# Weight splits written behind the chains of a tile, and five of 16 chunks of three modulation vectors moved from VectorE to TensorE's column groups

## The chip, the core and the metric

The kernel is one program on one core of a Trainium2 chip. The metric is the device time of one execution in microseconds, here the median of three runs. The engines have short names in the profile: PE is TensorE's matrix multiply and PEld its weight load, DVE is VectorE, ACT is ScalarE, POOL is GpSimd, SP issues the loads. Each engine works through its own queue of instructions in order. An instruction may wait for others by semaphores, and while it waits all that stand behind it on its engine wait too.

## What is computed

One layer of a network on 256 tokens of width 2048, in float32. Cut to what matters here:

```python
c_act = silu(c)
mod = c_act @ w_ada + b_ada                     # six vectors of 2048: 0 to 5
sh_m, sc_m, gt_m, sh_f, sc_f, gt_f = split(mod, 6)
h = rms_norm(x, g_norm_mix) * (1 + sc_m) + sh_m             # uses 1 and 0
b_g, c_g, h_c, q_lat, kv_lat, k_rope = split(h @ w_in)
conv_out = b_g * causal_conv3(c_g * h_c)
attn_out = mla_attention(q_lat, kv_lat, k_rope, ...)        # low-rank q and kv, 8 heads
merged = concat(group_rms_norm(conv_out), group_rms_norm(attn_out))
x = x + gt_m * (merged @ w_out)                             # uses 2
h2 = rms_norm(x, g_norm_ffn) * (1 + sc_f) + sh_f            # uses 4 and 3
x = x + gt_f * peer_ffn(h2)                                 # most of the time
return rms_norm(x, g_final)
```

## The kernel before

**Products.** A weight tile is 128 x 2048 numbers, 1 MB. It is split into a high part (`hi`, by ACT, line 198) and the rest (`lo`, by DVE, line 199), and a product is made of three: the high weights with the high and the low activations, then the low weights with the high activations (`mm3`, lines 213, 214 and 217). For a tile of 16 blocks that is a chain of 32 + 16 matmuls of 128 x 256. `load_split` does the load and the split. Its raw buffers (`wraw`, four) are shared with the chunks below; `hi` and `lo` have two buffers each, so that the split of a tile has to wait until the tile two before it has been used up: the `hi` buffer comes free two thirds into a chain, the `lo` buffer at its end.

**Stages.** The first 141 us make vectors 1 and 0 and the first twelve tiles of `w_in`, interleaved (`ada_q`, `unit`). Then come the tiles of the first convolution group, with the norms of the two latents between them (`lat_chain`: `ssl`, `rl0r`, `rlb0` for q, `ssl`, `rl1r`, `rlb1` for kv); the latent products `puq`, `puk`, `puv`; the mixer, 18 tiles `pwin` in six convolution groups (`conv_group`), with attention (`attend`) and the group norms (`conv_norm`: `cn0`, `cn1`) started at given tiles by `AGENDA` (the trace leaves numbers out: its `at_4pn` and `at_4on` are those of query half 1, heads 4 and 5); then `w_out`, 16 chains `pwout`, the first two interleaved with the norm `cn2`, each followed by its eviction (`wout_evict`) and scaling (`wout_scale`); the norm of the result (`x1ss`, `n1b`), and from 470 us on the query projection and the experts, which the diff doesn't touch. The tiles of a convolution group stand in the order 2, 3, 1 of it, so that the mixer's last three are tiles 19, 20 and 18.

**A norm** (`rstd_cols`, lines 340 to 349) is a row of short steps that go from PE's sums to DVE (`v`), to ACT (square root, `r`), and back to DVE for four steps (lines 345 to 348); PE then spreads the result (`rstd_bc`).

**Vectors 2, 4 and 3** come from `ada_stream`: 16 chunks each of 1 MB. Each chunk is multiplied with its 16th of `c_act` and added up on DVE in `acc` (`ada_acc`, line 241). After the last, four matmuls with ones sum over the partitions (`adaps`, in column groups of 32), ACT copies the row (`adarow`), four more matmuls turn it (`adacol`), and DVE adds the bias. `feed` takes one step of this stream whenever `PACE`, 46 chunks in 41 tiles, has added up to one, and it lets the waiting generators (norms, attention) go on by one step (`tick`).

**Order.** A scheduler orders each engine's instructions by the order in which they are written; `high_priority(offset=60)` in `load_split` moves the two split instructions ahead by that much.

Of the kernel before, what the change touches and what calls it, by code (L numbers as in the profile page):

```python
# [57 lines left out]
ADA_LAST = (0, 1, 1)  # L58
PACE = (48 - sum(ADA_LAST)) / 41.0
# [71 lines left out]
def hybrid_block_kernel(  # L131
# [100 lines left out]
    def ada_acc(acc, m, k, pool=None):  # L232
        if pool is None:
            raw = load_raw(w_ada[m - 2, k], f"ada{m}_{k}")
        else:
            raw = pool.tile([128, 2048], F32, tag="ar", name=f"ada{m}_{k}", bufs=ARBUFS)
            nc.sync.dma_start(raw, w_ada[m - 2, k])
# [4 lines left out]

    with tc.tile_pool(name="pre", bufs=1) as pre:
# [136 lines left out]
        pace = [0.0]  # L380
# [47 lines left out]

        def proj(src, nt, rhs, nm, sets=None):
# [3 lines left out]
            feed(PACE)  # L433
            return p[:, :256]
# [85 lines left out]
        def conv_group(g, ps=None):  # L520
# [8 lines left out]
            V.tensor_scalar(y, z[:, 0:256], vcol("conv_w", g), None, ALU.mult)  # L529
# [910 lines left out]
```

## Time and profile before

| | us |
|---|---|
| median of three runs | 1761.83 |
| the runs | 1760.68, 1761.83, 1767.35 |
| the profiled execution | 1762.56 |
| its span in the profile | 1760.8 |
| PE busy in it | 1683.4 |
| DVE busy | 1200.5 |
| ACT busy | 761.6 |

The profiled execution is the one in which the trace was taken; its span is the time from the first to the last recorded instruction, and what lies around it is 1.8 us. Busy time is the time in which an engine had an instruction at work. The idle time of an engine that isn't the bound costs nothing, so what counts is where PE stands idle, what it waited for, and what clock it had. PEclk is the granted share of the full clock: 1.00 is 2.4 GHz, 0.50 is 1.2 GHz.

### The profile page before, as it was taken

The numbers are of one execution on the slowest core, as the hardware profiler recorded it, in microseconds if no ns is written. First come the engines' busy times: TensorE is split into PE (matmuls) and PEld (weight loads), VectorE is DVE, ScalarE is ACT, GpSimd is POOL, SyncE is SP. The second block draws the span as 40 slices with busy tenths as digits, with TensorE's granted clock in tenths as the row PEclk, the third lists the DMA queues.
The fourth block names the chain that finished last, engine by engine and source line by source line (L and its number), as shares of the span: only waits on it lengthen the run. The fifth ranks groups of instructions, "written<-read, shape, count | busy, mean of one in ns | idle before, by whom it ended". The sixth has DMA issues, their size and how long they took to land. (4 is left out here: it accounts for less than half of the span.)

```text
span 1760.8 us, 29506 instructions
## 1 busy us (share of the span) xinstructions
PE 1683.4 (96%) x12507; PEld 1461.9 (83%) x12507; DVE 1200.5 (68%) x1605; ACT 761.6 (43%) x1016; POOL 288.1 (16%) x257
## 2 busy tenths in 40 slices
PE   4998999899999999999999999999999999999996
PEld 2778999899899999899999999999999754444542
DVE  6769899778667988897885788898744332222324
ACT  3233467334544468847974343333433232222322
POOL 0000000000000000000000000000030476756771
PEclk8988999899999999999999999999999999999998
DMA  9998888679555455546569887888988599998895
GB/s 396 425 375 298 324 331 304 244 277 348 207 217 180 158 182 212 195 175 219 198 233 347 284 307 255 296 298 286 322 311 317 219 393 393 354 361 336 307 395 217
DMA packets 77928, 505.93 MB, mean 287 GB/s; under 512 B 9472, under 2 KB 10112, under 8 KB 22496
## 3 DMA queue, kind: packets, MB, share of 16 engines
q1 hardware_dynamic: 44784, 319.82, 48.2%
q0 software_dynamic: 29712, 162.94, 25.3%
q10 hardware_dynamic: 3296, 21.24, 3.0%
q8 instruction: 100, 1.64, 0.4%
q14 instruction: 36, 0.29, 0.0%
HBM read 466.21 MB, written 37.75 MB: 286 GB/s over the span
## 5 line engine op out<-in xcount | busy, mean ns | idle before, releaser
L213 PE MATMUL pu<-h2hi,hu 128*128 128x256 f32 x2048 | 497.8, 284 | 0.0
L198 ACT ACTIVATE hu<-ru 128x2048 fp32r<-128x2048 f32 x128 | 245.4, 1917 | 365.7 <-PE pu L214 316.7
L213 PEld LDWEIGHTS pu<-h2hi,hu 128*128 128x128 f32 x2048 | 386.0, 188 | 0.6 <-issue 0.2
L199 DVE TENSOR_TENSOR lu<-ru,hu 128x2048 fp32r<-128x2048 f32 x128 | 293.1, 2291 | 135.6 <-ACT hu L198 133.4
L217 PE MATMUL pu<-h2hi,lu 128*128 128x256 f32 x2048 | 263.2, 281 | 0.5 <-DVE lu L199 0.5
L217 PEld LDWEIGHTS pu<-h2hi,lu 128*128 128x128 f32 x2048 | 251.3, 188 | 0.7 <-DVE lu L199 0.7
L214 PE MATMUL pu<-h2loT3a,hu 128*128 128x256 f32 x1024 | 249.4, 282 | 0.0
L214 PE MATMUL pu<-h2loT3b,hu 128*128 128x256 f32 x1024 | 247.9, 281 | 0.0
L1228 PE MATMUL po<-rv,mc 128*64 128x512 f32 (+2 forms) x1064 | 225.5, 600 | 5.2 <-PEq L1310 2.6
L1228 PEld LDWEIGHTS po<-rv,mc 128*64 128x64 f32 (+2 forms) x1064 | 72.6, 131 | 147.0 <-issue 140.5
L214 PEld LDWEIGHTS pu<-h2loT3a,hu 128*128 128x128 f32 x1024 | 193.2, 189 | 0.2 <-issue 0.2
L214 PEld LDWEIGHTS pu<-h2loT3b,hu 128*128 128x128 f32 x1024 | 192.9, 188 | 0.0
L1125 POOL DMA_DIRECT2D gg<-gd x16 | 18.7, 1169 | 914.9 <-DVE work L1002 914.6
L1170 POOL DMA_INDIRECT rv<-in_peer_v_dram,perm_idx x107 | 129.1, 1207 | 77.1 <-PE po L1228 33.2
L204 DVE TENSOR_TENSOR lv<-rv,hv 128x2048 fp32r<-128x2048 f32 x24 | 55.1, 2294 | 122.5 <-ACT hv L203 89.9
L1177 POOL DMA_INDIRECT mc<-actd,perm_idx x109 | 121.1, 1111 | 37.1 <-issue 30.8
L241 DVE SCALAR_TENSOR_TENSOR acc<-ada,cact,acc 128x2048 f32<-128x2048 f32 x45 | 105.7, 2348 | 3.4 <-DMA ada<-in_w_ada_dram 3.4
L203 ACT ACTIVATE hv<-rv 128x2048 fp32r<-128x2048 f32 x24 | 45.9, 1913 | 130.6 <-DMA rv<-in_peer_v_dram,perm_idx 118.4
L198 ACT ACTIVATE hwin<-rwin 128x2048 fp32r<-128x2048 f32 x33 | 63.0, 1910 | 66.1 <-DMA rwin<-in_w_in_dram 40.0
L213 PE MATMUL pwin<-hhi,hwin 128*128 128x256 f32 x336 | 88.4, 301 | 0.0
L872 ACT ACTIVATE oh<-oh,gT 128x128 f32<-128x128 f32 x256 | 80.8, 390 | 14.8 <-DVE oh L869 14.1
L204 DVE TENSOR_TENSOR third<-rv,third 128x2048 fp32r<-128x2048 f32 x12 | 27.6, 2299 | 87.3 <-ACT third L203 53.7
(522 smaller groups left out, 3036.3 us busy)
## 6 DMA issues: line engine op xcount, KB each, us to landing
ru<-in_peer_u_dram SPq DMA_DIRECT2D x128, 1024.0 KB, 5.4
ada<-in_w_ada_dram SPq DMA_DIRECT2D x96, 1024.0 KB, 7.4
rwin<-in_w_in_dram SPq DMA_DIRECT2D x33, 1024.0 KB, 6.1
rwout<-in_w_out_dram SPq DMA_DIRECT2D x16, 1024.0 KB, 5.3
rwq<-in_w_q_dram SPq DMA_DIRECT2D x16, 1024.0 KB, 4.8
gd<-stage ACTq DMA_DIRECT2D x16, 1024.0 KB, 5.0
gg<-gd POOLq DMA_DIRECT2D x16, 1024.0 KB
actd<-A POOLq DMA_DIRECT2D x15, 1024.0 KB
```

The lines of the kernel that those rows point to most:

```text
L198: S.activation(hi, raw, AF.Copy)
L199: V.tensor_tensor(lo, raw, hi.bitcast(F32), ALU.subtract)
L203: S.activation(hi, src, AF.Copy)
L204: V.tensor_tensor(lo, src, hi.bitcast(F32), ALU.subtract)
L213: PE.matmul(dst, lhsT=whi[:, sl], rhs=rhi[:, c], start=(c == sets[0][0]), stop=False)
L214: PE.matmul(dst, lhsT=whi[:, sl], rhs=rlo[:, c], start=False, stop=False)
L217: PE.matmul(dst, lhsT=wlo[:, sl], rhs=rhi[:, c], start=False, stop=(c == sets[-1][-1]))
L241: V.scalar_tensor_tensor(acc, raw, cact[:, k:k + 1], acc, ALU.mult, ALU.add)
L872: S.activation(ohs[1][:, j], ohs[1][:, j], AF.Copy, scale=gT[:, t + j:t + j + 1])
L1170: keep(nc.gpsimd.indirect_dma_start(raw, None, v_rows, index(main[n])))
L1177: keep(nc.gpsimd.indirect_dma_start(ms[-1][:, n % 8], None, actd[:, :], index(main[n])))
L1228: keep(PE.matmul(po[tt * 4 + d4][row:row + size], lhsT=m[:, at * size:(at + 1) * size], rhs=raw[:, d4 * 512:(d4 + 1) * 512], start=start, ...
```

## The change

**Chunks.** Of the 16 chunks of each vector, the five in `ADA_PE3` are no longer multiplied on DVE. PE does them in the four column groups of the tile `adaps`, four matmuls of 128 x 512 a chunk, and the sum of the other eleven (`acc` times ones) is added into the same tile. That tile is one of eight PSUM buffers and is now held from the vector's beginning to its end. The pace goes by stage, and one chunk less is taken before the first convolution tiles.

**Splits.** The tiles after the first stage stand in a list (`todo`), and `split_next`, called in `feed` behind a chain and behind `tick`, writes the next load and split, two tiles ahead, with no offset in the order.

**Moved steps.** The first tap of the convolution and the scaling by `r` in attention go from DVE to ACT; the square of the last `w_out` column goes from ACT to DVE.

```diff
-ADA_LAST = (0, 1, 1)
-PACE = (48 - sum(ADA_LAST)) / 41.0
+ADA_LAST = (0, 0, 1)
+ADA_PE3 = (2, 5, 8, 11, 14)
+PACES = {"start": 0.67, "latent": 1.0, "mixer": 1.1, "out": 1.4}
...
-        def ada_finish(m, acc):
-            p = ps_tile(f"adaps{m}")
-            by_columns(p, ones[:, 0:32], acc, True, True)
+        def ada_finish(m, acc, p):
+            by_columns(p, ones[:, 0:32], acc, stop=True)
...
                 acc = t8(f"acc{m}", shape=(128, 2048))
+                p = ps_tile(f"adaps{m}")
                 for k in range(16):
-                    ada_acc(acc, m, k, pre if ARBUFS else None)
+                    raw = load_raw(w_ada[m - 2, k], f"ada{m}_{k}")
+                    if k in ADA_PE3:
+                        by_columns(p, cact[:, k:k + 1].to_broadcast([128, 32]), raw, start=(k == ADA_PE3[0]))
+                    else:
+                        ada_acc(acc, raw, k)
...
-        def feed(x):
+        def feed(n=1, ahead=1):
             tick()
-            pace[0] += x
+            for _ in range(ahead):
+                split_next()
+            pace[0] += n * pace[1]
...
+        def split_next():
+            if todo:
+                src, j, nm = todo.pop(0)
+                ready.append((src, j, load_split(src[j], f"{nm}{j}", 0)))
...
         def proj(src, nt, rhs, nm, sets=None):
-            w = load_split(src[nt], f"{nm}{nt}")
+            w = weights(src, nt)
...
-            V.tensor_scalar(y, z[:, 0:256], vcol("conv_w", g), None, ALU.mult)
+            S.activation(y, z[:, 0:256], AF.Copy, scale=vcol("conv_w", g))
...
-                V.tensor_scalar(on[:, gs_], po[:, gs_], r[:, g:g + 1], None, ALU.mult)
+                S.activation(on[:, gs_], po[:, gs_], AF.Copy, scale=r[:, g:g + 1])
...
         conv_group(0, [pin_nt(9 + i) for i in range(3)])
+        split_next()
+        split_next()
         conv_group(1)
...
-            S.activation(sq[:, :256], xt[:, dt], AF.Square)
+            if dt == 15:
+                V.tensor_tensor(sq[:, :256], xt[:, dt], xt[:, dt], ALU.mult)
+            else:
+                S.activation(sq[:, :256], xt[:, dt], AF.Square)
...
-                feed(2 * PACE)
+                feed(2, 0)
+        for dt in range(2):
+            split_next()
```

The order of the instructions shows the effect at three places. The first is DVE at the norm of the q latent, behind the last chains of the first stage; `lwin` is the low half of a tile's split, `acc` a chunk, `z` the convolution's product. Before:

```order
L199 TENSOR_TENSOR lwin_1226<-rwin_1223,hwin_1225 128x2048 [waits DMAHW5_49,Activation_49]
L345 RECIPROCAL rl0r<-rl0r 128x2 [waits Activation_49]
L472 TENSOR_TENSOR krT<-kraw,rope_t 128x256 [waits Activation_49]
L346 SCALAR_TENSOR_TENSOR rl0v<-rl0v,rl0r 128x2 [waits DVE_49]
L526 MEMSET z_1215 128x2
L241 SCALAR_TENSOR_TENSOR acc_1136<-ada_2_1295,cact,acc_1136 128x2048 [waits DMAHW6_49]
L347 TENSOR_TENSOR rl0v<-rl0v,rl0r 128x2 [waits DVE_49]
L527 TENSOR_TENSOR z_1215<-cs_1213,pin_179 128x256 [waits Activation_49]
L348 SCALAR_TENSOR_TENSOR rl0r<-rl0v,rl0r 128x2 [waits DVE_49]
```

After, on DVE at the same place (line numbers of the changed kernel):

```order
L342 TENSOR_SCALAR rl0v<-ssl_1116 128x2 [waits PE_49]
L200 TENSOR_TENSOR lwin_1223<-rwin_1220,hwin_1222 128x2048 [waits DMAHW4_49,Activation_49]
L345 RECIPROCAL rl0r<-rl0r 128x2 [waits Activation_49]
L475 TENSOR_TENSOR lacc_1130<-lsq_1129 128x256 [waits Activation_49]
L346 SCALAR_TENSOR_TENSOR rl0v<-rl0v,rl0r 128x2 [waits DVE_49]
L494 TENSOR_TENSOR krT<-kraw,rope_t 128x256 [waits Activation_49]
L347 TENSOR_TENSOR rl0v<-rl0v,rl0r 128x2 [waits DVE_49]
L476 TENSOR_TENSOR lacc_1130<-lacc_1130 128x256
L348 SCALAR_TENSOR_TENSOR rl0r<-rl0v,rl0r 128x2 [waits DVE_49]
```

Before, a chunk stands between the second and the third step of `rl0r`; now no chunk and no split stands between its steps on DVE behind the reciprocal.

The second place is DVE at the norm `cn1`, in the mixer's last group. `lwin_3277` before and `lwin_3221` after are the low half of the same tile, 18; its buffer is that of tile 19, whose chain is the last on PE ahead of `cn1b`. Before:

```order
L199 TENSOR_TENSOR lwin_3206<-rwin_3203,hwin_3205 128x2048 [waits DMAHW4_49,Activation_49]
L639 SCALAR_TENSOR_TENSOR mg1lo<-at_6pn,vec,mg1hi 128x128 [waits Activation_49]
L345 RECIPROCAL cn1r<-cn1r 128x4 [waits Activation_49]
L346 SCALAR_TENSOR_TENSOR cn1v<-cn1v,cn1r 128x4 [waits DVE_49]
L347 TENSOR_TENSOR cn1v<-cn1v,cn1r 128x4 [waits DVE_49]
L639 SCALAR_TENSOR_TENSOR mg1lo<-at_6pn,vec,mg1hi 128x128 [waits Activation_49]
L348 SCALAR_TENSOR_TENSOR cn1r<-cn1v,cn1r 128x4 [waits DVE_49]
L199 TENSOR_TENSOR lwin_3277<-rwin_3274,hwin_3276 128x2048 [waits DMAHW6_49,PE_49,Activation_49]
```

After, on DVE at the same place:

```order
L345 RECIPROCAL cn1r<-cn1r 128x4 [waits Activation_49]
L237 SCALAR_TENSOR_TENSOR acc_2453<-ada_10_3224,cact,acc_2453 128x2048 [waits DMAHW1_49,DVE_49]
L346 SCALAR_TENSOR_TENSOR cn1v<-cn1v,cn1r 128x4 [waits DVE_49]
L200 TENSOR_TENSOR lwin_3221<-rwin_3218,hwin_3220 128x2048 [waits DMAHW0_49,PE_49,Activation_49]
L347 TENSOR_TENSOR cn1v<-cn1v,cn1r 128x4 [waits DVE_49]
L548 MEMSET z_3289 128x2
L348 SCALAR_TENSOR_TENSOR cn1r<-cn1v,cn1r 128x4 [waits DVE_49]
L527 SCALAR_TENSOR_TENSOR ym<-ym,vec,cn1b_3209 128x256 [waits PE_49]
```

The split stood behind the last step of `cn1r`, and now stands ahead of its last two.

The third place is ACT at the end of `w_out`. `hwout12` to `hwout15` are the high halves of the last splits, `xs1` the scaling of a column (`xs` in the trace), `x1sq` its square. A scaling that waits for DVE waits for an eviction (`xt`). Before:

```order
L745 ACTIVATE xs1_3343<-xt_97,modc_76 128x256
L738 ACTIVATE x1sq11_4117<-xt_97 128x256 [waits DVE_49]
L745 ACTIVATE xs1_3343<-xt_97,modc_76 128x256
L198 ACTIVATE hwout13_4198<-rwout13_4196 128x2048 [waits DMAHW4_49,PE_49,Activation_49]
L306 ACTIVATE adarow3_4188<-adaps3_4183 128x512 [waits PE_49]
L738 ACTIVATE x1sq12_4191<-xt_97 128x256 [waits DVE_49]
L745 ACTIVATE xs1_3343<-xt_97,modc_76 128x256
L198 ACTIVATE hwout14_4265<-rwout14_4263 128x2048 [waits DMAHW5_49,Activation_49]
L198 ACTIVATE hwout15_4326<-rwout15_4324 128x2048 [waits DMAHW6_49,DVE_49,PE_49]
L738 ACTIVATE x1sq13_4258<-xt_97 128x256 [waits DVE_49]
```

After, on ACT at the same place:

```order
L768 ACTIVATE x1sq11_4172<-xt_97 128x256 [waits DVE_49]
L775 ACTIVATE xs1_3356<-xt_97,modc_76 128x256
L775 ACTIVATE xs1_3356<-xt_97,modc_76 128x256 [waits DVE_49]
L199 ACTIVATE hwout13_4164<-rwout13_4162 128x2048 [waits DMAHW1_49,PE_49,Activation_49]
L199 ACTIVATE hwout14_4228<-rwout14_4226 128x2048 [waits DMAHW3_49,PE_49,Activation_49]
L775 ACTIVATE xs1_3356<-xt_97,modc_76 128x256 [waits DVE_49]
L199 ACTIVATE hwout15_4310<-rwout15_4308 128x2048 [waits DMAHW6_49,PE_49,Activation_49]
L301 ACTIVATE adarow3_4245<-adaps3_3579 128x512 [waits PE_49]
L768 ACTIVATE x1sq12_4248<-xt_97 128x256
L768 ACTIVATE x1sq13_4315<-xt_97 128x256
```

`hwout13` stood behind the scaling of column 8 or 9 and now stands behind one that waits for the eviction of chain 12; `adarow3` stood behind `hwout13` and now stands behind `hwout15`. On PE, `adaps3` stood behind chain 12 and `adacol3` behind chain 13; now eight matmuls of `adaps3` (chunk 14 and the finish) stand behind chain 13, and `adacol3` directly behind them, ahead of chain 14. On PE the eight matmuls of `adaps4` now stand between `cn2b` and the first product of the norm, where before nothing stood.

## Rows read from the trace of the kernel before

**Rows 1.** The page: busy us, share of the span, instructions of each engine.

```profile
PE 1683.4 (96%) x12507; PEld 1461.9 (83%) x12507; DVE 1200.5 (68%) x1605; ACT 761.6 (43%) x1016; POOL 288.1 (16%) x257
```

**Rows 2.** Windows of PE: stretch, us, busy of five engines, PEclk, DMA share, GB/s.

```profile
143.75:150.57 6.82, 6.64 (x31) 6.68 (x32) 6.24 (x12) 1.15 (x2) 0.00 (x0) 0.50 0.62 227
157.40:160.81 3.41, 3.41 (x18) 3.41 (x17) 3.41 (x8) 0.68 (x1) 0.00 (x0) 0.50 0.95 372
250.00:300.00 50.00, 50.00 (x416) 49.59 (x416) 47.24 (x75) 32.79 (x68) 0.00 (x0) 1.00 0.83 308
311.01:317.83 6.82, 6.82 (x34) 6.82 (x34) 5.62 (x14) 2.01 (x9) 0.00 (x0) 0.50 1.01 410
324.65:331.48 6.83, 5.69 (x26) 5.72 (x27) 6.39 (x12) 1.01 (x2) 0.00 (x0) 0.50 0.73 270
372.44:379.27 6.83, 5.70 (x28) 5.40 (x27) 6.83 (x6) 4.30 (x4) 0.00 (x0) 0.50 0.58 208
```

**Rows 3.** Timeline of PE: start, us, engine, line, operation, tiles, count, [idle before <-releaser].

```profile
143.93 1.20 PE L354 MATMUL rlb<-ident,rl0r 128*128 128x128 f32 x4 [2.67 <-DVE rl0r L348]
...
156.41 0.68 PE L354 MATMUL rlb<-ident,rl1r 128*128 128x128 f32 x4 [2.65 <-DVE rl1r L348]
...
178.08 0.70 PE L469 MATMUL qr10sw<-qraw,perm 128*128 128x256 f32 x2 [1.15 <-ACT qraw L546]
...
310.00 0.33 PE L634 MATMUL at_4pn<-ident,at_4on 128*128 128x128 f32 x1 [2.37 <-DVE at_4on L626]
...
325.79 1.62 PE L354 MATMUL cn0b<-ident,cn0r 128*128 128x128 f32 x6 [3.82 <-DVE cn0r L348]
...
370.66 0.50 PE L754 MATMUL pwout<-mg0hi,hwout 128*128 128x256 f32 x2 [1.63 <-ACT mg0hi L203]
...
460.69 0.60 PE L337 MATMUL x1ss<-ones,sacc 128*128 128x1 f32 x4 [3.11 <-DVE sacc L742]
```

**Rows 4.** Timeline of DVE ahead of `rl0r`'s last steps.

```profile
140.96 2.35 DVE L241 SCALAR_TENSOR_TENSOR acc<-ada,cact,acc 128x2048 f32<-128x2048 f32 x1
```

**Rows 5.** Timeline of DVE ahead of `cn0b`.

```profile
322.81 2.28 DVE L199 TENSOR_TENSOR lwin<-rwin,hwin 128x2048 fp32r<-128x2048 f32 x1
325.01 0.16 DVE L347 TENSOR_TENSOR cn0v<-cn0v,cn0r 128x8 f32<-128x8 f32 x1
...
325.49 0.16 DVE L348 SCALAR_TENSOR_TENSOR cn0r<-cn0v,cn0r 128x8 f32<-128x8 f32 x1
```

**Rows 6.** Timeline of ACT ahead of `cn0r`'s square root.

```profile
320.12 1.92 ACT L198 ACTIVATE hwin<-rwin 128x2048 fp32r<-128x2048 f32 x1 [6.60 <-PE pwin L214]
```

**Rows 7.** Timeline of PE: the group of `adaps` between two chains of `w_out`.

```profile
438.58 1.07 PE L299 MATMUL adaps<-acc,ones 128*32 128x512 f32 x8
439.57 0.39 PE L213 MATMUL pwout<-mg0hi,hwout 128*128 128x256 f32 x1
439.80 0.28 PE L214 MATMUL pwout<-mg0lo,hwout 128*128 128x256 f32 x1
```

**Rows 8.** Timeline of DVE: evictions in `w_out`, each at the end of its chain.

```profile
404.93 0.48 DVE L736 SCALAR_TENSOR_TENSOR xt<-pwout,modc,xt 128x256 f32<-128x256 f32 x1 [0.34 <-PE pwout L217]
...
410.56 0.48 DVE L736 SCALAR_TENSOR_TENSOR xt<-pwout,modc,xt 128x256 f32<-128x256 f32 x1 [0.34 <-PE pwout L217]
...
438.69 0.48 DVE L736 SCALAR_TENSOR_TENSOR xt<-pwout,modc,xt 128x256 f32<-128x256 f32 x1 [0.28 <-PE pwout L217]
...
445.49 0.48 DVE L736 SCALAR_TENSOR_TENSOR xt<-pwout,modc,xt 128x256 f32<-128x256 f32 x1 [0.34 <-PE pwout L217]
```

**Rows 9.** Timeline of ACT in `w_out`.

```profile
439.71 0.60 ACT L306 ACTIVATE adarow<-adaps 128x512 f32<-128x512 f32 x1 [3.50 <-PE adaps L299]
...
440.51 0.50 ACT L745 ACTIVATE xs<-xt,modc 128x256 f32<-128x256 f32 x1
440.91 1.91 ACT L198 ACTIVATE hwout<-rwout 128x2048 fp32r<-128x2048 f32 x1
```

**Rows 10.** The page's DMA issues: KB each, us from issue to landing.

```profile
ada<-in_w_ada_dram SPq DMA_DIRECT2D x96, 1024.0 KB, 7.4
```

More of the change, by code (lines that the diff above doesn't have):

```diff
@@ L230, in rstd_of, with ada_acc @@
         return r
[L232 to L237, printed above, removed]
+    def ada_acc(acc, raw, k):
         if k == 0:
@@ L379, in hybrid_block_kernel @@
         ada = ada_stream((2, 4, 3))
-        pace = [0.0]
-        def feed(x):
+        pace = [0.0, PACES["start"]]
+        def feed(n=1, ahead=1):
             tick()
-            pace[0] += x
+            for _ in range(ahead):
+                split_next()
+            pace[0] += n * pace[1]
             while pace[0] >= 1.0:
@@ L427, in ada_q, with tiles, groups, weights @@
                 yield
+        def tiles():
+            def groups(gs):
+                return [(w_in, 3 * g - 3 + i, "win") for g in gs for i in (1, 2, 0)]
+            return (groups((1,)) + [(w_uq, j, "wuq") for j in (2, 0, 1)] + [(w_ukv, j, "wukv") for j in range(4)] +
+                    groups(range(2, 8)) + [(w_out, j, "wout") for j in range(16)])
+        todo = tiles()
+        ready = []
+        def split_next():
+            if todo:
+                src, j, nm = todo.pop(0)
+                ready.append((src, j, load_split(src[j], f"{nm}{j}", 0)))
+        def weights(src, j):
+            got = ready.pop(0)
+            assert got[0] is src and got[1] == j
+            return got[2]
         def proj(src, nt, rhs, nm, sets=None):
-            w = load_split(src[nt], f"{nm}{nt}")
+            w = weights(src, nt)
             p = ps_tile(f"p{nm}{nt}")
             mm3(p[:, :256], w, rhs, 16, sets=sets)
-            feed(PACE)
+            feed()
             return p[:, :256]
@@ L534, in uq_tile @@
         def uq_tile(j):
-            w = load_split(w_uq[j], f"wuq{j}")
+            w = weights(w_uq, j)
             for n2 in range(2):
@@ L548, in uq_tile @@
                         spawn(rope(qrT[:, i0 - 8 + i], raw[:, i * 256:(i + 1) * 256], f"qr{i0 + i}"))
-            feed(PACE)
+            feed()
         def uk_tile(j):
-            w = load_split(w_ukv[j], f"wuk{j}")
+            w = weights(w_ukv, j)
             for n2 in range(2):
@@ L559, in uk_tile @@
                 S.activation(knT[:, i0:i0 + 2], pv, AF.Copy)
-            feed(PACE)
+            feed()
         def uv_tile(j):
-            whi, wlo = load_split(w_ukv[2 + j], f"wuv{j}")
+            whi, wlo = weights(w_ukv, 2 + j)
             for tt in range(2):
@@ L574, in uv_tile @@
                 S.activation(vt[:, tt, j * 512:(j + 1) * 512], p, AF.Copy)
-            feed(PACE)
+            feed()
         ATT_SCALE = float(192 ** -0.5)
@@ L717, in hybrid_block_kernel @@
         vt = pre.tile([128, 2, 1024], F32, tag="t8", name="vt", bufs=6)
+        pace[1] = PACES["latent"]
         for j in (2, 0, 1):
@@ L725, in hybrid_block_kernel @@
         agenda.update(AGENDA(attend, conv_norm))
+        pace[1] = PACES["mixer"]
         for g in range(2, 8):
             conv_group(g)
+        pace[1] = PACES["out"]
         drain()
@@ L745, in wout_scale @@
             S.activation(xs1[:, dt], xt[:, dt], AF.Copy, scale=modc[:, 4, dt:dt + 1])
-        ws = [load_split(w_out[dt], f"wout{dt}") for dt in range(2)]
+        ws = [weights(w_out, dt) for dt in range(2)]
         pw = [ps_tile(f"pwout{dt}") for dt in range(2)]
```

2 lines of the change are left out of this document (1 added, 1 removed).

## The prediction

> **What bounds the kernel now.** I read the busy shares first: PE is busy for 96% of the span [rows 1], so work given to PE is paid in full unless it falls into a wait of PE. The changed code ends at the query projection, 470 us into the program; behind it nothing moves. So I read the stretch from 140 to 470 us by its windows. In a window like 250 to 300 us PE is busy for all 50 us at a clock of 1.00 [rows 2]: no relief of DVE or ACT can gain anything there. What can be gained lies in two things. First the waits: the timeline of PE shows four that the change touches, 2.67 us before `rlb0`, 2.37 before `at_4pn`, 3.82 before `cn0b`, 1.63 before the first `mg0hi` product, together 10.5 us [rows 3]. Second, what follows each: at or just behind each of these waits stands a stretch of 6.8 us with PEclk 0.50, which is the lower of the two levels (1.2 GHz). PE is busy in these for 6.64, 6.82, 5.69 and 5.70 us [rows 2], and half of that is lost: 3.3 + 3.4 + 2.8 + 2.9 = 12.4 us. The wait of 1.15 us before `qr10sw` [rows 3] has no such stretch behind it.
>
> All these waits have one form: a short DVE or ACT step that PE waits for stands in its engine's queue behind a long one. Before `rlb0` it is a chunk of the modulation stream, 2.35 us [rows 4]. Before `cn0b`, ACT's split `hwin` stood idle 6.60 us for a buffer [rows 6], with the square root of `cn0r` behind it, and then DVE's `lwin` (322.81 to 325.01) stood ahead of `cn0r`'s last steps [rows 5].
>
> **What the change takes away.** By the order of the changed kernel, no chunk and no split stands any more between the last steps of `rl0r`, the product of `at_4on` is on ACT, `cn0r`'s root stands ahead of the split on ACT, and the wait at `cn2b` holds eight matmuls of `adaps4`. I take all four waits as gone, with the stretches behind them: 10.5 + 12.4 = 22.9 us gained. The 15 chunks that leave DVE free 15 x 2.35 = 35 us of it, but beyond the four waits that buys nothing, since PE doesn't wait there. The first tap of the convolution and the attention products cost ACT what they free on DVE; neither is late for PE elsewhere, so I put them at nothing. The loads on SP are as many as before, and the finish of each vector (a group of `adaps`, four `adacol`) is paid in both kernels.
>
> **What it adds on PE.** 15 groups of four matmuls. The trace has three groups of this form, `adaps`, there with the ones vector. The group at 438.58 us is followed at 439.57 by the next chain, 0.99 us later, and that chain's second matmul comes 0.23 us behind its first, where 0.12 is usual (a chain of 48 in 5.63 us) [rows 7, 8]: 1.1 us a group. The other measure is DVE's evictions: from one chain to the next 5.63 us (404.93 to 410.56), and 6.80 (438.69 to 445.49) with a group between [rows 8], so 1.17. The ends are 15 x 1.0 = 15.0 and 15 x 1.17 = 17.6 us; I take 15 x 1.1 = 16.5. A gain is excluded, as PE has no other wait for them to lie in but the one at `cn2b`, counted above.
>
> The Trainium skill (TensorEngine Tiling (Array Packing), Key Properties) says that a change of tiling mode, not just of tile, drains the TensorE; that speaks against groups set in among full-width chains. The trace agrees as far as the 0.1 us behind the group goes. If the drain were two whole matmuls of 0.28 us in place of 0.12, the groups would cost 15 x 1.3 = 19.8 us, and the sum would be 3 us more.
>
> **What it adds as waits.** The splits are now written right behind the chain before, so that some stand ahead of short steps where before they stood behind them.
> - `cn1b`: DVE's `lwin` of tile 18 waits for the end of chain 19 (its buffer), and `cn1r`'s last two steps now stand behind it; `cn1b` is next on PE. In rows 5 the same row of steps runs from `lwin`'s start at 322.81 to `cn0r` at 325.49 with one other step in it, and 0.30 later PE goes on [rows 3]. So 2.7 us idle (2.3 to 3.2).
> - Chain 13 of `wout`: ACT's `hwout13` stands behind a scaling that waits for the eviction of chain 12. Eviction about 0.5 [rows 8], scaling to split 0.40 and the split 1.91 [rows 9], a hand-over of 0.1: 2.9 us idle (2.4 to 3.5).
> - Behind chain 13: `adaps3`'s last group needs the chunk 15 on DVE, which stands behind the eviction (0.4), `lwout14` (2.3 [rows 5]) and takes 2.35 itself: 5.0 us. Then the group 1.0, `adarow` 0.13 later and 0.60 long [rows 7, 9], then `adacol`, which PE now has ahead of chain 14: 6.8 us, of which 2.1 are work (chunk 14 and the finish). So 4.7 us idle. In the kernel before, a whole chain lay between `adaps3` and `adacol`. ACT has `hwout15`, which waits for its load, ahead of `adarow`: 4.0 to 6.5.
> - `rlb1`: idle 2.65 now [rows 3]. With `rlb0` on time, DVE has two splits (2.3 each), four latent products (0.5 each, like an eviction), a low half of about 1.2 by the split's rate, a first chunk (at most 2.35) and small steps to do, 10 to 11 us, against a chain of 5.6 and 1.1 of small products on PE: 3.3 to 4.3. I take 3.9, 1.2 more.
> - `x1ss` [rows 3]: the square of column 15 now stands on DVE behind `lwq`, ahead of the sum: 0.4 more.
>
> That is 2.7 + 2.9 + 4.7 + 1.2 + 0.4 = 11.9 us idle. The waits of 2.37 us and more in rows 3 each have a stretch at the lower level: 3.1 us lost in the mean of four, 1.7 where another had ended 7 us before (157.40 [rows 2]). For `cn1b` and chain 13 I take 3.0 each, for the end of `wout`, close behind chain 13, 1.7, and 1.3 more at `rlb1`, which loses its near neighbour: 9.0 us (0 to 12).
>
> **The sum.** 16.5 + 11.9 + 9.0 - 22.9 = +14.5 us on the profiled execution's 1762.56, thus 1777; this execution is 0.7 us over the median of the runs, so 1776. Its own range, from the ends of the terms, is 1771 to 1782.
>
> **The rivals.**
> - The clock stays up at the new waits. For it: the 1.15 us before `qr10sw` left it at 1.00. Against: each wait over 2.3 us in rows 3 has its stretch. Then 9.0 us less: 1767, no change that can be told. It decides from the point where two of the three new places keep the clock: 6 us less is 1770. This is the one that ends on the other side, not slower.
> - The new waits are shorter than the order says, because DVE and ACT, with 35 us less on DVE, come to those places early and only the buffer's release counts. Without them, idle and clock, 20.9 us less: 1755; with groups at 1.0 us and a little more, under 1753. Against: the step that counts in each waits for PE's own chain, so an early engine gains nothing.
> - PE waits for loads. Now 15 places of PE, not of DVE, wait for a chunk; a chunk takes 7.4 us to land [rows 10], the DMA share is already 0.83 at 250 to 300 us [rows 2], and one PSUM buffer of eight is held all the time. At half a microsecond a place, +8: 1784. Against: the chunk's load is issued a tile or more ahead.
> - The change doesn't free the short steps: some other long step is still ahead of `rl0r`, `at_4on` or `cn0r`. Half of the 22.9 not gained: 1788.
> - The drain as the page has it: 1780.
>
> **How the numbers follow.** Forecast 0.45, clock stays up 0.18, shorter waits 0.17, loads 0.12, no freeing 0.05, drain 0.03. A measurement of this kernel tells about 0.5%, 8.8 us, from no change, thus under 1753 and over 1770.6. Faster: 0.10, the better part of the shorter waits. Same: their rest 0.07, the clock's 0.18 and 0.03 of the forecast, 0.28. Slower: 0.62. The range 1755 to 1785 leaves out the faster part and the dearest cases, some 0.15.
>
> **What would show it.** Right: PE without idle before `rlb0`, `at_4pn` and `cn0b`; idle of 2 to 4 us before `cn1b` and before chain 13, and some 4 us before `adaps3`'s last group and `adacol`; PEclk 0.50 behind these; 15 groups of `adaps` a chunk at 1.0 to 1.2 us from start to next; everything behind the query projection as long as before. Wrong: idle before `adaps` groups released by a DMA, the old waits still there, or a clock of 1.00 behind the new ones.

## The result: 0.9% slower

The changed kernel takes 1775.92 us in the median of ten runs (1768.79 to 1784.24); the kernel before, run beside it, 1761.09 (1756.73 to 1767.35). The ratio is 1.0086, with a 95% interval of 1.0070 to 1.0102. The forecast was 1776, between 1755 and 1785. The profiled execution has a span of 1775.8 us, 15.0 over that of before.

The page of the changed kernel (columns as in [rows 1]) shows PE busy for 12 us more and DVE for 38 us less:

```profile
PE 1695.8 (95%) x12622; PEld 1458.1 (82%) x12627; DVE 1162.4 (65%) x1567; ACT 770.3 (43%) x1039; POOL 290.2 (16%) x257
```

Where the time comes and goes is seen best in the starts of PE's steps on both timelines:

| first step of | before, us | after, us | after minus before |
|---|---|---|---|
| latent norm `ssl` | 134.97 | 136.67 | +1.70 |
| latent products `puq` | 170.25 | 167.77 | -2.48 |
| attention `at_0s` | 212.66 | 211.74 | -0.92 |
| norm `cn0ss` | 311.32 | 312.44 | +1.12 |
| norm `cn1ss` | 336.20 | 328.78 | -7.42 |
| norm `cn2b` | 367.91 | 362.59 | -5.32 |
| norm `x1ss` | 460.69 | 475.36 | +14.67 |
| query projection `pq` | 469.17 | 482.58 | +13.41 |
| span | 1760.8 | 1775.8 | +15.0 |

At `cn2b` the changed kernel is 5.3 us ahead; from there to `x1ss`, in `w_out`, it loses 20.0. That is the place where the sum is decided.

The timeline of PE after (columns as in [rows 3], where six of these steps stand for before). The rows without brackets are `rlb0`, `at_4pn`, `cn0b` and the first `mg0hi` product, now without a wait. An `x8` of `adaps` is one group of four matmuls:

```profile
142.79 0.61 PE L354 MATMUL rlb<-ident,rl0r 128*128 128x128 f32 x4
...
153.05 1.19 PE L354 MATMUL rlb<-ident,rl1r 128*128 128x128 f32 x4 [3.53 <-DVE rl1r L348]
...
311.33 0.38 PE L656 MATMUL at_4pn<-ident,at_4on 128*128 128x128 f32 x2
...
319.91 1.28 PE L354 MATMUL cn0b<-ident,cn0r 128*128 128x128 f32 x10
...
338.28 0.93 PE L354 MATMUL cn1b<-ident,cn1r 128*128 128x128 f32 x6 [2.77 <-DVE cn1r L348]
...
365.43 0.51 PE L784 MATMUL pwout<-mg0hi,hwout 128*128 128x256 f32 x2
...
382.76 1.06 PE L295 MATMUL adaps<-ada,cact 128*32 128x512 f32 x8 [1.60 <-DMA ada<-in_w_ada_dram]
...
441.14 0.39 PE L214 MATMUL pwout<-mg0hi,hwout 128*128 128x256 f32 x1 [2.92 <-ACT hwout L199]
...
453.61 1.94 PE L295 MATMUL adaps<-acc,ones 128*32 128x512 f32 x8 [4.04 <-DVE acc L237]
456.26 1.02 PE L305 MATMUL adacol<-quad,adarow 128*128 128x4 f32 x4 [0.72 <-ACT adarow L301]
...
475.36 0.61 PE L337 MATMUL x1ss<-ones,sacc 128*128 128x1 f32 x4 [3.57 <-DVE sacc L772]
```

The wait before `rlb1` grew from 2.65 to 3.53 us. New are those before `cn1b` (2.77), chain 13 (441.14, 2.92), the last group of `adaps3` and `adacol3` (4.04 + 0.72), and one before a group at 382.76 that waited 1.60 us for its chunk to land. The one before `x1ss` grew from 3.11 to 3.57.

What stands ahead of them is as the order says. DVE at `cn1b`: the split's low half starts when chain 19 has ended (335.52) and ACT's high half, which the row names, a tenth of a microsecond later, and it holds up the last two steps of `cn1r`.

```profile
334.40 0.15 DVE L346 SCALAR_TENSOR_TENSOR cn1v<-cn1v,cn1r 128x4 f32<-128x4 f32 x1
335.67 2.29 DVE L200 TENSOR_TENSOR lwin<-rwin,hwin 128x2048 fp32r<-128x2048 f32 x1 [1.11 <-ACT hwin L199]
337.87 0.16 DVE L347 TENSOR_TENSOR cn1v<-cn1v,cn1r 128x4 f32<-128x4 f32 x1
...
338.06 0.16 DVE L348 SCALAR_TENSOR_TENSOR cn1r<-cn1v,cn1r 128x4 f32<-128x4 f32 x1
```

ACT ahead of chain 13: the scaling waited 5.92 us for the eviction of chain 12 (`xt`), and `hwout13` came behind it.

```profile
438.78 0.51 ACT L775 ACTIVATE xs<-xt,modc 128x256 f32<-128x256 f32 x1 [5.92 <-DVE xt L763]
439.20 1.89 ACT L199 ACTIVATE hwout<-rwout 128x2048 fp32r<-128x2048 f32 x1
```

DVE behind chain 13: eviction, split, and only then chunk 15, which the last group of `adaps3` needs.

```profile
448.60 0.48 DVE L763 SCALAR_TENSOR_TENSOR xt<-pwout,modc,xt 128x256 f32<-128x256 f32 x1 [2.93 <-PE pwout L218]
449.00 2.28 DVE L200 TENSOR_TENSOR lwout<-rwout,hwout 128x2048 fp32r<-128x2048 f32 x1
451.20 2.35 DVE L237 SCALAR_TENSOR_TENSOR acc<-ada,cact,acc 128x2048 f32<-128x2048 f32 x1
```

A group inside a chain (chain 6 of `w_out`), on the timeline of PE: 0.21 us from the matmul before to the group, 0.99 from the group to the next matmul, 0.23 to the one after. Without the group these three distances would be 0.12, none and 0.12, so the group costs 1.2 us.

```profile
398.37 0.28 PE L214 MATMUL pwout<-mg1hi,hwout 128*128 128x256 f32 x1
398.58 1.06 PE L295 MATMUL adaps<-ada,cact 128*32 128x512 f32 x8
399.57 0.38 PE L215 MATMUL pwout<-mg1lo,hwout 128*128 128x256 f32 x1
399.80 0.28 PE L214 MATMUL pwout<-mg1hi,hwout 128*128 128x256 f32 x1
```

The windows with the clock (columns as in [rows 2]): the lower level at `rlb1`, behind the wait before chain 13, and for 10.2 us around the end of `adaps3`. Behind the wait before `cn1b`, 2.77 us of idle, the clock stayed at 1.00.

```profile
152.58:156.00 3.42, 2.95 (x12) 2.80 (x13) 3.42 (x6) 0.00 (x0) 0.00 (x0) 0.52 1.02 410
338.00:345.00 7.00, 6.72 (x56) 6.63 (x56) 3.47 (x7) 2.31 (x2) 0.00 (x0) 1.00 0.51 190
442.59:446.00 3.41, 3.41 (x18) 3.41 (x18) 3.09 (x2) 1.13 (x1) 0.00 (x0) 0.50 0.62 202
452.83:463.06 10.23, 8.74 (x40) 7.01 (x41) 3.91 (x5) 2.63 (x4) 0.00 (x0) 0.50 0.89 345
```

### The profile page after: what moved, and what is told of

It is laid out like the page before. It is cut to its first block, busy times and chain, and to the rows that moved or that the text cites. A ratio compares the mean times of both kernels' runs of the same rounds, so it can differ in the third digit from the quotient of the medians.

```text
span 1775.8 us, 29725 instructions
## 1 busy us (share of the span) xinstructions
PE 1695.8 (95%) x12622; PEld 1458.1 (82%) x12627; DVE 1162.4 (65%) x1567; ACT 770.3 (43%) x1039; POOL 290.2 (16%) x257
## 5 line engine op out<-in xcount | busy, mean ns | idle before, releaser
L1209 POOL DMA_INDIRECT mc<-actd,perm_idx x109 | 131.9, 1210 | 37.1 <-issue 31.4
L1202 POOL DMA_INDIRECT rv<-in_peer_v_dram,perm_idx x107 | 120.4, 1125 | 76.3 <-PE po L1260 30.6
L200 DVE TENSOR_TENSOR lwin<-rwin,hwin 128x2048 fp32r<-128x2048 f32 x33 | 75.5, 2289 | 25.5 <-ACT hwin L199 17.8
L199 ACT ACTIVATE hwin<-rwin 128x2048 fp32r<-128x2048 f32 x33 | 63.1, 1912 | 52.1 <-PE pin L688 22.9
L214 PE MATMUL pwin<-hhi,hwin 128*128 128x256 f32 x336 | 83.2, 289 | 0.0
```

The source lines that it names most:

```text
L199: S.activation(hi, raw, AF.Copy)
L200: V.tensor_tensor(lo, raw, hi.bitcast(F32), ALU.subtract)
L214: PE.matmul(dst, lhsT=whi[:, sl], rhs=rhi[:, c], start=(c == sets[0][0]), stop=False)
L1202: keep(nc.gpsimd.indirect_dma_start(raw, None, v_rows, index(main[n])))
L1209: keep(nc.gpsimd.indirect_dma_start(ms[-1][:, n % 8], None, actd[:, :], index(main[n])))
```

## The experiments

Medians; the ratio is that to the kernel before, measured beside it, with its 95% interval. The kernel before had medians of 1761.53 us beside e1 to e4, 1759.11 beside e5 to e8 and 1760.04 beside e9 to e11, so that kernels of different groups are better compared by their ratios, and 0.001 is 1.8 us.

| run | what is changed | us | ratio |
|---|---|---|---|
| after | all of it | 1775.92 | 1.0086 (1.0070 to 1.0102) |
| e1 | after, without groups | 1769.37 | 1.0039 (1.0018 to 1.0060) |
| e2 | after, each group twice | 1784.23 | 1.0129 (1.0108 to 1.0150) |
| e3 | before, with the groups alone | 1761.15 | 0.9996 (0.9984 to 1.0008) |
| e4 | before, with the moved steps alone | 1753.08 | 0.9949 (0.9933 to 0.9965) |
| e5 | before, with moved steps and splits | 1774.10 | 1.0083 (1.0068 to 1.0099) |
| e6 | after, pace 1.5 in `w_out` | 1771.52 | 1.0071 (1.0056 to 1.0086) |
| e7 | after, norm steps ahead of splits | 1763.97 | 1.0031 (1.0019 to 1.0043) |
| e8 | e4, steps of group norms ahead | 1748.22 | 0.9945 (0.9932 to 0.9959) |
| e9 | after, splits of `w_out` as before | 1767.89 | 1.0046 (1.0030 to 1.0062) |
| e10 | e7 and e9, four groups | 1746.08 | 0.9923 (0.9907 to 0.9939) |
| e11 | e7 and e9, ten groups | 1750.46 | 0.9940 (0.9921 to 0.9959) |

**e1: no groups.**

```diff
-ADA_PE3 = (2, 5, 8, 11, 14)
+ADA_PE3 = ()
```

> The changed kernel with all 48 chunks on DVE again (the set of chunks for PE is empty); the new place of the splits, the moved steps and the paces by stage stay. My theory (PE is full, a group of four matmuls costs 1.1 us, DVE's relief earns nothing outside its waits): 16.5 us less for the groups, and the waits before chain 13 and adacol3 go too, since chunk 14 and 15 then stand elsewhere in the order; cn1b and rlb1 keep theirs (2 to 4 us each). About 1752 us, thus 22 to 26 below the changed kernel. Rival A (the groups are nearly free and the splits' place is the loss): 1768 to 1775. Rival B (the loss is PE waiting for chunk loads): only some 2 to 8 us less than the changed kernel.

1769.37 us, 6.6 below the changed kernel (8.3 by the ratios) and not the 22 to 26 that I had expected. The time alone fits both rivals; the trace shows another cause. Up to `cn2b` it is 11.0 us ahead of before, 5.7 more than the changed kernel. Then it loses 20.5 in `w_out`, nearly all at one step of PE:

```profile
446.10 1.94 PE L295 MATMUL adaps<-acc,ones 128*32 128x512 f32 x8 [15.62 <-DVE acc L237]
```

With a pace of 1.4 chunks a tile, the splits and all chunks on DVE, DVE had more to do in this stage than PE: it was busy for 63.1 of the 72 us from 363 to 435 and fell behind, and `adaps3` waited for it for 15.62 us. I had read the order for what stands ahead of whom, but not added up DVE's work by stage: 1.4 x 2.35 + 2.29 + 0.48 + 0.42 is 6.5 us a tile, against 5.63 of a chain [rows 4, 5, 8].

**e2: each group twice.**

```diff
                         by_columns(p, cact[:, k:k + 1].to_broadcast([128, 32]), raw, start=(k == ADA_PE3[0]))
+                        by_columns(p, zero32, raw)
```

> The changed kernel with a second group of four matmuls behind each of the 15, on the same chunk with zero weights, so that nothing is added to the sum. My theory: 15 x 1.0 to 1.1 us more, 15 to 16.5, minus what falls into a wait (the wait at cn2b holds one more). About 1790 us. Rival A (groups nearly free): under 5 us more. A dearer drain at each change of tiling mode (the page's rule) isn't doubled here, since both groups stand side by side: a group by itself would then cost clearly more than the second one adds, 1.3 against 1.0.

1784.23, 8.3 us over the changed kernel. One pair on PE's timeline:

```profile
168.42 1.06 PE L297 MATMUL adaps<-ada,cact 128*32 128x512 f32 x8
169.30 1.04 PE L297 MATMUL adaps<-ada,zero 128*32 128x512 f32 x8
170.28 0.39 PE L216 MATMUL puq<-lathi,hwuq 128*128 128x256 f32 x1
```

From its start to the next product the pair takes 0.88 + 0.98 = 1.86 us, where a single group takes 0.99 (398.58 to 399.57 above). So the second group adds 0.87 us, less than the 1.0 to 1.1 expected. The starts of PE's steps say the same: from the first `puq` to the first `at_6pt`, the last attention block, e2 takes 142.76 us (170.28 to 313.04) and the changed kernel 137.45 (167.77 to 305.22), with six doubled groups between, 0.89 each. A group by itself costs 1.2 us, so what the two switches cost, ahead of it and behind it, is about 0.3, and a pair pays that once. That is the difference of 1.3 against 1.0 that the expectation gives for the dearer drain.

Fifteen second groups are 13 us by this price. Some of that fell into waits: the one at `cn1b` was 0.92 where it had been 2.77, and the one before chain 13 was gone, with its low stretch.

**e3: the groups alone.** The chunks' lines of the diff, put into the kernel before; one pace, splits and steps as before.

```diff
+ADA_PE3 = (2, 5, 8, 11, 14)
...
                 for k in range(16):
-                    ada_acc(acc, m, k, pre if ARBUFS else None)
+                    if k in ADA_PE3:
+                        raw = load_raw(w_ada[m - 2, k], f"ada{m}_{k}")
+                        by_columns(p, cact[:, k:k + 1].to_broadcast([128, 32]), raw, start=(k == ADA_PE3[0]))
+                    else:
+                        ada_acc(acc, m, k)
```

> The kernel before with only the 15 chunks moved to PE; splits, steps and the one pace as before. My theory: 16.5 us more on PE; by the order of it the wait before rlb0 goes (6.0 us with its stretch of lower clock), the one before at_4pn too (5.8), those of cn0b and mg0hi shrink by what the groups now in them take; rlb1 stays. About 1764 us (1760 to 1768). Rival A (groups nearly free, the relief of DVE pays): 1750 or less.

1761.15, no difference from before (ratio 0.9996). That is inside the 1760 to 1768 expected, but not by the steps expected: `at_4pn` has no wait left, `rlb0` shrank only to 1.09, `cn0b` to 1.88, and `rlb1` grew to 4.59.

```profile
141.34 0.68 PE L359 MATMUL rlb<-ident,rl0r 128*128 128x128 f32 x4 [1.09 <-DVE rl0r L353]
...
152.73 1.19 PE L359 MATMUL rlb<-ident,rl1r 128*128 128x128 f32 x4 [4.59 <-DVE rl1r L353]
...
324.96 1.33 PE L359 MATMUL cn0b<-ident,cn0r 128*128 128x128 f32 x8 [1.88 <-DVE cn0r L353]
```

So fifteen groups at 1.2 us were paid back, in the waits that DVE's chunks had made and more still in the clock. PE's idle from 140 to 376 us is 5.7 us less than before (9.9 for 15.6), and half of PE's busy time in low stretches, from 135 to 470 us, is 6.2 us where it was 16.9. The rival (1750 or less) is out.

**e4: the moved steps alone.** The first tap and the attention scaling on ACT, in the kernel before.

```diff
-            V.tensor_scalar(y, z[:, 0:256], vcol("conv_w", g), None, ALU.mult)
+            S.activation(y, z[:, 0:256], AF.Copy, scale=vcol("conv_w", g))
...
-                V.tensor_scalar(on[:, gs_], po[:, gs_], r[:, g:g + 1], None, ALU.mult)
+                S.activation(on[:, gs_], po[:, gs_], AF.Copy, scale=r[:, g:g + 1])
```

> The kernel before with only the first tap of the convolution and the attention scaling moved from DVE to ACT. My theory: by its order rlb0 and rlb1 no longer stand behind a chunk or a split, and at_4pn less; cn0b, mg0hi and x1ss stay. rlb0 6.0, rlb1 4.3, at_4pn up to 5.8 us: 1745 to 1752 us. Rival: the clock's stretches come anyway, so only the idle of 5 to 7 us is gained: 1754 to 1756.

1753.08, 0.5% below before and between the 1745 to 1752 expected and the rival's 1754 to 1756. The wait at `rlb0` stayed, against what I expected; those at `rlb1` and `at_4pn` shrank to 0.28 and 0.42.

```profile
143.92 1.20 PE L354 MATMUL rlb<-ident,rl0r 128*128 128x128 f32 x4 [2.67 <-DVE rl0r L348]
...
154.02 0.68 PE L354 MATMUL rlb<-ident,rl1r 128*128 128x128 f32 x4 [0.28 <-DVE rl1r L348]
...
303.34 0.33 PE L634 MATMUL at_4pn<-ident,at_4on 128*128 128x128 f32 x1 [0.42 <-ACT at_4on L626]
...
315.84 1.44 PE L354 MATMUL cn0b<-ident,cn0r 128*128 128x128 f32 x5 [3.70 <-DVE cn0r L348]
```

**e5: the splits, without groups.** The new place of the splits and the moved steps, all chunks on DVE, one pace of 46/41. Against the changed kernel:

```diff
-ADA_LAST = (0, 0, 1)
-ADA_PE3 = (2, 5, 8, 11, 14)
-PACES = {"start": 0.67, "latent": 1.0, "mixer": 1.1, "out": 1.4}
+ADA_LAST = (0, 1, 1)
+ADA_PE3 = ()
+PACES = dict.fromkeys(("start", "latent", "mixer", "out"), (48 - 2) / 41.0)
```

> The kernel before with the moved steps and the splits written behind the chains, two tiles ahead, but no groups on PE and the one pace of before (46 chunks in 41 tiles). Beside e4 (the moved steps alone, 1753) it differs in the place of the splits (and the square of column 15). My theory: the splits' place itself makes waits, since DVE's low halves wait in the queue for a chain's end: by the order rlb1 (3.5 us and its stretch of lower clock, 1.7), cn1b (2.7), and adaps3 behind chain 12, which has an eviction, a split and two chunks ahead of it on DVE (7.4 us and a stretch of 3), minus rlb0's 6.0. About 12 us over e4: 1765. Rival: the place is harmless, as DVE has room with no groups to serve: 1753, as e4.

1774.10. The place of the splits costs 0.0134 of the time, some 23 us over e4, twice what I had expected (0.5 of it is the square of the last column, which also moved to DVE, at `x1ss`). The waits:

```profile
234.85 1.94 PE L295 MATMUL adaps<-acc,ones 128*32 128x512 f32 x8 [5.02 <-DVE acc L237]
...
327.23 1.01 PE L355 MATMUL cn0b<-ident,cn0r 128*128 128x128 f32 x3 [5.95 <-DVE cn0r L349]
...
347.08 1.22 PE L355 MATMUL cn1b<-ident,cn1r 128*128 128x128 f32 x4 [2.57 <-DVE cn1r L349]
...
451.62 1.94 PE L295 MATMUL adaps<-acc,ones 128*32 128x512 f32 x8 [7.42 <-DVE acc L237]
```

Two that I had not listed are 5.02 us at `adaps2` and 5.95 at `cn0b`: in both the step that PE waits for stands on DVE behind chunks or a split that itself came late. This is the decisive run: the splits' place makes the loss. Which half of that edit does it, two tiles ahead or no offset in the order, this run doesn't tell.

The time is that of the changed kernel (the ratios differ by 0.0003), which has the groups and the paces by stage besides. Run e1 has the paces without the groups, and it parts the two: its ratio is 0.0044 below that of e5, and neither of these waits is there. `adaps2` and `cn0b` in e1:

```profile
249.45 1.06 PE L295 MATMUL adaps<-acc,ones 128*32 128x512 f32 x8
...
315.08 1.95 PE L355 MATMUL cn0b<-ident,cn0r 128*128 128x128 f32 x16
```

So the paces by stage (with the one chunk less at the start) take back some 8 us of the splits' 23, and the groups on top of them cost 8 (0.0047, e1 against the changed kernel).

**e6: one number.**

```diff
-PACES = {"start": 0.67, "latent": 1.0, "mixer": 1.1, "out": 1.4}
+PACES = {"start": 0.67, "latent": 1.0, "mixer": 1.1, "out": 1.5}
```

> The changed kernel with one number changed: the pace of the last stage 1.5 a tile where it is 1.4. By the order chunks 14 and 15 of vector 3 then come early enough that adaps3's last group no longer waits for an eviction and a split on DVE, and hwout13 no longer stands behind the scaling of column 12. My theory: the idle of 2.9 and 4.0 us goes with the two stretches of lower clock there (1.7 and 2.9), 0.7 to 1 stays at adacol: 10 to 11 us less than the changed kernel, about 1765. Rival: PE is behind its loads in this stage, and the waits only move to chunk loads: within 4 us of the changed kernel.

1771.52, 4.4 us below the changed kernel by the medians and 2.6 by the ratios, whose intervals overlap. The 10 to 11 us expected are out. The waits before chain 13 and `adaps3` became shorter but stayed where they were, and the one at `adacol3` grew; none of the three is for a load, as the rival has it:

```profile
441.91 0.38 PE L214 MATMUL pwout<-mg0hi,hwout 128*128 128x256 f32 x1 [2.29 <-ACT hwout L199]
...
451.48 1.94 PE L295 MATMUL adaps<-acc,ones 128*32 128x512 f32 x8 [2.49 <-DVE acc L237]
454.57 1.66 PE L305 MATMUL adacol<-quad,adarow 128*128 128x4 f32 x7 [1.15 <-ACT adarow L301]
```

Up to `w_out` this kernel is written as the changed one is, and its wait before `cn1b` is the same 2.77 us. But here the clock fell behind it (a mean of 0.76 in the window in which it had stayed at 1.00):

```profile
338.56 1.82 PE L354 MATMUL cn1b<-ident,cn1r 128*128 128x128 f32 x8 [2.77 <-DVE cn1r L348]
```

```profile
338.00:345.00 7.00, 6.44 (x41) 6.44 (x42) 4.03 (x8) 0.63 (x1) 0.00 (x0) 0.76 0.56 208
```

**e7: the norms' short steps ahead.** The seven instructions of `rstd_cols`, indented under one line:

```diff
+            with tc.high_priority(offset=200):
...
             v = small(nm + "v", 8)[:, :k]
```

> The changed kernel with the short steps of every norm put ahead of the splits in the order (a priority of 200 for their seven instructions). By the order rlb1 and cn1b then stand a whole chain away from what they need; the end of w_out is as in the changed kernel. My theory: rlb1 3.5 us and its stretch of lower clock (1.7), cn1b 2.8 without one: 8 us less, about 1768. Rival: the time is given back in the next stage, because DVE and ACT come later to the splits that are now behind: within 3 us of the changed kernel.

1763.97, 12 us below the changed kernel by the medians and 10 by the ratios; 8 were expected. `rlb1` and `cn1b` have no wait at all, as the row of `cn1b` shows, and nothing was given back: at `cn2b` it is 12.84 us ahead of before, where the changed kernel is 5.32. At the query projection the two profiles differ by 7.9 us; what goes beyond that lies in a stage that the edit doesn't touch.

```profile
330.67 1.05 PE L355 MATMUL cn1b<-ident,cn1r 128*128 128x128 f32 x8
```

**e8: the kernel before with such steps ahead.** The moved steps of e4, and the priority of e7 for `cn0`, `cn1`, `cn2` and for the eviction of the last column.

```diff
+            with tc.high_priority(offset=200 if nm.startswith("cn") else 0):
...
             v = small(nm + "v", 8)[:, :k]
...
-            wout_evict(dt, p)
+            with tc.high_priority(offset=200 if dt == 15 else 0):
+                wout_evict(dt, p)
```

> The kernel before with the moved steps of e4, the short steps of the group norms and the eviction of the last w_out column put ahead of the splits; no groups on PE, splits and pace as before. My theory: beside e4 (1753) the wait of cn0b falls from 3.7 to about 1 us and that of x1ss from 3.1 to about 1.4, with their stretches of lower clock at least in part: 4 us of idle and 0 to 6 of clock: 1743 to 1749. Rival: the split that is pushed back delays the next chain by as much: 1752 to 1754.

1748.22, inside the expected range, but not for the expected reason: both waits are still there. At `cn0b` the root still stands on ACT behind `hwin`, which waited 3.63 us for its buffer, and the last two steps of `cn0r` behind `lwin` on DVE (312.07, 2.29 us). At `x1ss` (3.11 us, as before) the split for the query projection still stands ahead of the sum.

```profile
315.03 1.26 PE L355 MATMUL cn0b<-ident,cn0r 128*128 128x128 f32 x8 [3.77 <-DVE cn0r L349]
```

By the ratio to before it is no faster than e4 (0.9945 and 0.9949). This one tells nothing of the mechanism.

**e9: the splits of `w_out` where they were.** `weights` calls `load_split` with its old offset for tiles of `w_out`, which `tiles` no longer lists.

```diff
         def weights(src, j):
+            if src is w_out:
+                return load_split(src[j], f"wout{j}")
```

> The changed kernel, but the 16 tiles of w_out are loaded and split where they were before, ahead by 60 in the order and directly ahead of their chain; the pace of 1.4 and the groups stay. My theory: the loss at the end of w_out is that of the splits' place: the idle before chain 13, adaps3 and adacol (7.7 us) goes, with its stretches of lower clock (4.6), and one or two us come at chains 8, 11 and 13, whose splits have a group's length or two as cover. 8 us less than the changed kernel, about 1767. Rival: the pace of 1.4 is the cause (too many chunks in this stage, whoever does them): within 3 us of the changed kernel.

1767.89, 8 us below by the medians and 7 by the ratios, as expected and more than the rival's 3. The waits at the end of `w_out` are gone; three at chains 8, 11 and 13 (1.06 us) have come, the first two a little longer than I had put them:

```profile
410.32 0.38 PE L214 MATMUL pwout<-mg0hi,hwout 128*128 128x256 f32 x1 [2.23 <-ACT hwout L199]
...
432.25 0.39 PE L214 MATMUL pwout<-mg0hi,hwout 128*128 128x256 f32 x1 [2.23 <-ACT hwout L199]
```

**e10 and e11: a version that gains.** Norm steps ahead as in e7, splits of `w_out` as in e9, no groups for vector 3. In e10 two chunks of vectors 2 and 4 on PE, in e11 five, with paces of 1.1 and 1.12 in the last two stages. e10 against the changed kernel:

```diff
-ADA_PE3 = (2, 5, 8, 11, 14)
+ADA_PE3 = {2: (5, 10), 4: (5, 10), 3: ()}
-PACES = {"start": 0.67, "latent": 1.0, "mixer": 1.1, "out": 1.4}
+PACES = {"start": 0.67, "latent": 1.0, "mixer": 1.2, "out": 1.1}
```

> The changed kernel with the short steps of every norm ahead of the splits (as in e7), the splits of w_out as in e9, the last column's eviction ahead too, only two chunks (5 and 10) of vectors 2 and 4 on PE, none of vector 3, and paces 1.2 in the mixer and 1.1 in w_out. My theory: only waits of under 1.5 us are left on PE but for x1ss, and four groups cost 4 us: against before 2.7 + 2.6 + 2.4 + 3.8 us of idle less and most of 11 us of clock, about 1743. Rival: DVE, with 44 chunks left to it, falls behind in the mixer, where the pace is higher, and the waits of e5 come back: 1755 or more.

> As e10, but all five chunks of vectors 2 and 4 on PE (ten groups), the mixer's pace 1.1 and w_out's 1.12. My theory: with the waits gone in both, six groups more cost 6 us: about 1749. Rival: the relief of DVE is what keeps the waits away: below e10.

In both kernels the eviction of the last column was left in its old order, unlike the words of the expectation. e10 takes 1746.08 us (1743 expected), 0.8% below before; e11 1750.46 (1749 expected). Whether e10 beats e8 or e11 is not settled by these intervals. From 130 to 440 us e10 keeps the clock at 1.00 (mean) and PE busy for 301.6 of 310 us; in the kernel before these were 0.95 and 294.4. The two windows, e10 first:

```profile
130.00:440.00 310.00, 301.61 (x2477) 290.72 (x2475) 261.36 (x303) 166.52 (x250) 0.00 (x0) 1.00 0.84 317
```

```profile
130.00:440.00 310.00, 294.36 (x2297) 286.55 (x2296) 266.36 (x322) 148.11 (x216) 0.00 (x0) 0.95 0.81 303
```

The waits of over 1.5 us that are left in e10 behind 130 us are one for a chunk's load, one for a split of `w_out`, and that at `x1ss` (3.13):

```profile
181.69 1.06 PE L295 MATMUL adaps<-ada,cact 128*32 128x512 f32 x8 [1.86 <-DMA ada<-in_w_ada_dram]
...
426.86 0.38 PE L214 MATMUL pwout<-mg0hi,hwout 128*128 128x256 f32 x1 [1.66 <-ACT hwout L199]
```

e11 lies 4.4 us over e10 by the medians. Its six groups more are 5 to 7 us on PE, at 0.87 to 1.2 each, but its paces differ too.

## Why the prediction was right, and where its steps were not

The total was right, and every wait that was forecast stood in its place. Term by term, on the profiled executions:

| term | forecast, us | measured, us | from |
|---|---|---|---|
| 15 groups | +16.5 | +17 to 18 | 1.2 each at thirteen places |
| four waits gone | -10.5 | -10.5 | no idle at `rlb0`, `at_4pn`, `cn0b`, `mg0hi` |
| their low stretches | -12.4 | -12.4 | none at these places |
| `cn1b` idle | +2.7 | +2.77 | timeline |
| chain 13 idle | +2.9 | +2.92 | timeline |
| `adaps3` and `adacol3` idle | +4.7 | +4.76 | timeline |
| `rlb1` idle | +1.2 | +0.88 | 3.53 - 2.65 |
| `x1ss` idle | +0.4 | +0.46 | 3.57 - 3.11 |
| new low stretches | +9.0 | about +4.5 | below |
| a wait for a load | 0 | +1.60 | 382.76 |
| the first stage | 0 | +1.7 | `ssl` |
| behind `pq` | 0 | +1.6 | 15.0 - 13.41 |

**The waits.** All five sizes held within 0.4 us. They were made of durations from rows of before and of what stands ahead in the order, and this is the part that carries over.

**The clock** was mis-sized: 9.0 us forecast, about 4.5 found. Half of PE's busy time in the low stretches gives 1.7 before chain 13 and 4.4 at the end of `adaps3`, no change at `rlb1` (1.5 against 1.7 before), and 1.4 less at `x1ss` than before. At `cn1b`, where I had taken 3.0, there was none, though the wait of 2.77 us is longer than the 2.37 and 2.67 before `at_4pn` and `rlb0` that had theirs. The step that failed is the sentence that waits of 2.37 us and more each have a stretch. Thus the first rival was half true. That the total came out within a microsecond is luck: the 4.5 us too many stand against 4.9 that were not forecast, 1.6 for a load, 1.7 in the first stage and 1.6 behind `pq`.

**The groups** cost 1.2 us each and not 1.1. I had seen the tenth of a microsecond behind the group and missed the one ahead of it. e2 tells the parts apart: 0.87 for a group beside another, so about 0.3 for the two switches. The Trainium skill (TensorEngine Tiling (Array Packing), Key Properties) says that a change of tiling mode drains the TensorE. The 0.3 us agree with such a drain. My estimate of the dearer switches, from two whole matmuls, was as large, but I had added it to 0.99 us that already held a tenth of it, and so came to 1.3 a group.

**DVE's relief.** "Beyond the four waits that buys nothing" was wrong. In the kernel before, the relief bought about what the groups cost (e3). In the changed kernel the groups cost 8 us net of 17 to 18 (e1), as without them `adaps3` waits 15.62 us for DVE and not 4.04. The forecast had also left out the waits of 5 to 6 us that the splits' new place makes at `adaps2` and `cn0b` (e5), and the paces by stage, which remove them (e1). These omissions cancel. So the forecast had the right time and in part the wrong culprit: it put 16.5 us down to the groups and about 21 to new waits, less 22.9 for the old ones. By the ratios, one edit upon the other, the moved steps gain 9 us (e4), the splits' place costs 23 to 24 (e5), the paces give back 8 (e1), and the groups cost 8.

**The loads.** One group waited for its chunk, 1.60 us; the rival had put half a microsecond at each of 15 places. At the others the chunk was there.

**Not in the forecast** were 1.7 us in the first stage, where the low stretch of the clock ran from 26.1 to 43.2 us and not from 31.1 to 41.4, with hardly anything changed in the order. e6, which is written the same there, has 6.8 us of low clock at this place and `ssl` at 135.48, and the profiles of the other runs have `ssl` between 133.96 and 137.08, so this is not assigned to the change. Nor are the 1.6 us behind `pq`, where both kernels have the same instructions in the same order. What remains open is why one wait is followed by the lower clock and another isn't: the same 2.77 us before `cn1b` had it in e6 and not in the changed kernel.

## What to carry to other kernels

Before a bulk step is written earlier, look at what the order puts behind it: a short step that the bound engine waits for must not stand behind an instruction that waits for that engine's own work; priority for the seven instructions of a norm was worth some 10 us here (e7). Then add up each engine's work by stage beside the order, since a stage in which a second engine becomes full waits at its end (e1). Work given to a full engine can still be paid back where it shortens what others wait behind; how much depends on the kernel that it is put into (all of it in e3, about half in the changed kernel), and only each edit run alone tells.

## What was not expected of the hardware

- The lower clock does not follow the length of a wait alone: 2.37 us before `at_4pn` had a stretch of 6.8 us behind it, 2.77 before `cn1b` none, 2.92 before chain 13 one of 3.4, and 4.04 at `adaps3` one of 10.2. Nor is it settled by the wait and its place: behind 3.53 us before `rlb1` the stretch was 3.4 us in the changed kernel and in e1, and 6.8 in e2, e6 and e9; behind 2.92 us before chain 13 there was none in e7. So what the clock takes at one and the same wait differs by some 1.7 us from run to run, as half of PE's busy time in 3.4 us.
- The last stage, from the first `po` to the end, has the same instructions in every kernel here and took 373.2 us before and 373.8 after, but 377.0 in e4 and 367.2 in e8. So a difference of 5 us between the spans of two single profiles of this kernel says nothing.
